# The order of the first two weight tiles in a seven-product FFN kernel: both P6 ahead of both P7, and the third tile's first sum made by a transfer

## The chip, the cores and the metric

The kernel runs on one core of one Trainium2 chip. Its time is the device time of one execution in microseconds (us); lower is better. A kernel's time is the median of several executions. One execution of it was recorded by the hardware profiler, and the trace of that one gives all durations, waits and starts below. Starts in the trace are counted from the beginning of the profiled span.

## What is computed

One decoder layer on a sequence of 1024 rows of 1024 numbers (float32): a pooling mixer, then a feed-forward network with a short causal convolution. Cut to what the change touches, the reference is:

```python
def conv_ffn(x, w_in, conv_w, conv_b, w_out):
    h = causal_depthwise_conv(x @ w_in, conv_w, conv_b)   # 3 taps
    val, gate = jnp.split(h, 2, axis=-1)
    return (jax.nn.silu(gate) * val) @ w_out

x = x + pool_mixer(rms_norm(x, norm_mix_g), ...)
x = x + conv_ffn(rms_norm(x, norm_ffn_g), ...)
```

x is 1024 by 1024, w_in 1024 by 5632 (2816 values and 2816 gates), w_out 2816 by 1024. The change touches only the product with w_in and what follows it up to the gated result.

## The kernel before, in words

**Stages.** First the pooling mixer and the norms (rows of x in eight blocks, up to some 75 us of the span). Then the product with w_in: 22 weight tiles n = 0 to 21, each of 128 value columns and the 128 gate columns that belong to them; the result of each tile is gated and written to HBM (`g_dram`). Last the product with w_out (L722 on).

**Seven products in place of eight.** A weight tile is a 2 by 2 block matrix (A11, A12 for the value columns, A21, A22 for the gate columns; each 128 by 512), and the normed rows are one as well (B11 to B22). The kernel uses a Strassen-Winograd scheme: sums S1 to S4 of the tile's blocks, sums T1 to T4 of the rows' blocks, and seven products P1 to P7 (the table STEPS, L421). Each takes one A side and one B side into one PSUM bank:

P1 = A11, B11 (bank X); P6 = S2, T2 (Y); P5 = S1, T1 (Z); P2 = A12, B21 (X, added to P1); P7 = S3, T3 (Y, added to P6); P3 = S4, B22 (Z, added to P5); P4 = A22, T4 (Y, added again).

Every float32 operand is split in a high and a low part (`split`, L91, for the A side: a copy on ACT at L93, then a subtraction on DVE at L94; `split_n`, L351, for the B side, the same at L353 and L354). One product is 12 matmuls on TensorE (PE): four pieces of 128 rows by three pairs of parts (`product`, L413).

**Evictions.** Between the products of one tile, DVE reads the banks (`step`, L430): q2 = Y after P6 minus q1 (L447), half of `hb` = r minus Y after P7 (L455), the other half = q1 minus Y after P4 (L460), `ha` from Z and q2 (L449). A product that adds to a bank can't start before DVE has read what it needs of the bank's state: P7 of a tile waits for its q2, P4 for its first half of `hb`. The tile `hb` (the gate half, 128 by 1024) has one buffer (L454, bufs=1), and so has `ha` (the value half).

**Gating** (`conv` L462, `gated` L472). For `ha` and then `hb`: one ACTIVATE on ACT (L465) and two SCALAR_TENSOR_TENSOR on DVE (L466, L467, the second on the first's output); then Silu on ACT (L476), a multiplication on DVE (L477) and a write to HBM.

**Weight sums** (`sums_in` L373, `prep_in` L391). A tile's raw weights are loaded into one of two `win` buffers by one 1 MB transfer on SP's queue (L362), which must wait until the tile two before it has made its last split, that of A22. S3 starts as another load of A11 (L381). Then GpSimd's queue (POOL) issues transfers that add in flight (L376): first A21 onto S3, then A22 onto A21 (which gives S1). S2 is A11 + S1, in place of A11: tiles 0 and 1 get it by a transfer too, all others by one addition on DVE (L368 by way of L399). S4 is A12 + S2.

**What sets the order.** The list `events` (L480 to L482) is the order in which products are asked for; `prep_event(k + LOOK)` asks for the operand splits five events ahead. A scheduler in the recording layer turns the program into one fixed queue for each engine, and each queue is worked off in order. For tiles 0 and 1 the list interleaves, since T2, T3 and T4 become ready only while these tiles are multiplied (L596 to L609); from tile 2 on it runs tile by tile in the order of STEPS.

Of the kernel before, what the change touches and what calls it, by code (L numbers as in the profile page):

```python
# [11 lines left out]
ALU = mybir.AluOpType  # L12
# [35 lines left out]
NH = 512  # L48
# [4 lines left out]
def woven(t):  # L53
    return t.rearrange("p (a b) -> p b a", a=2)
# [6 lines left out]
def halved(t, n=2):  # L61
    return t.rearrange("p (a b) -> p a b", a=n)
# [3 lines left out]
def trunk_kernel(ctx: ExitStack, tc: tile.TileContext, x, consts, par, rows, pool_w, w_in, w_out, out):  # L66
# [47 lines left out]
    def affine(t, src, op, fill, base, pattern, step):  # L114
        nc.gpsimd.affine_select(out=t, in_=src, compare_op=op, fill=fill, base=base, pattern=pattern, channel_multiplier=step)
# [21 lines left out]
    for g, w in enumerate(WINDOWS):  # L137

        m = band[:, g, :]
# [28 lines left out]
    marks = {}  # L168
# [153 lines left out]
    nops = {}  # L322
# [28 lines left out]
    def split_n(t, src, cols=None, ks=slice(None)):  # L351
        h, l = (t[:, i, ks] if cols is None else t[:, i].rearrange("p k (a s) -> p k a s", a=2)[:, :, :, cols] for i in range(2))
        hi = nc.scalar.activation(h, src, AF.Copy).ins  # L353
        return hi, nc.vector.tensor_tensor(l, src, h.bitcast(F32), ALU.subtract).ins  # L354
# [3 lines left out]
    raws, sums, aops = {}, {}, {}  # L358
# [11 lines left out]
    def tmp(name):  # L370
        return work.tile([P, NH], F32, tag="sum", name=name, bufs=3)

    def sums_in(n, step):  # L373

        def more(out, a):
            nc.gpsimd.dma_start(out, a, accum_op=ALU.add)  # L376

        a11, a12, a21, a22 = (raws[n][:, i, k * NH : (k + 1) * NH] for i in range(2) for k in range(2))
        if step == 0:
            s3 = sums[n, "S3"] = tmp(f"S3_{n}")  # L380
            nc.sync.dma_start(s3, w_in[order[n]][:, 0, :NH])  # L381
            more(s3, a21)
        if step == 0 and n > 1 or step == 2:
            more(a21, a22)
        if step == 1:
            sums[n, "S2"] = a11
            more(a11, a21)
            sums[n, "S4"] = a12
            more(a12, a11)

    def prep_in(n, op):  # L391
        a11, a12, a21, a22 = (raws[n][:, i, k * NH : (k + 1) * NH] for i in range(2) for k in range(2))
        if op in ("S1", "S2") and (n, "S3") not in sums:
            s3 = sums[n, "S3"] = tmp(f"S3_{n}")
            add(s3, a11, a21)
            add(a21, a21, a22)
        if op in ("S2", "S4") and (n, "S2") not in sums:
            sums[n, "S2"] = a11
            add(a11, a21, a11)  # L399
        if op == "S4" and (n, "S4") not in sums:  # L400
            add(a12, a12, a11)
        if op == "S3":
            src = sums[n, "S3"]
        else:
            src = {"A11": a11, "A12": a12, "S1": a21, "A22": a22, "S2": a11, "S4": a12}[op]
        log = []
        aops[n, op] = split(src, f"{op}s_{n}", log)
        marks[op, n] = log[0]
        if op == "A22" and n + 2 < NF:
            load_in(n + 2)  # L410
            sums_in(n + 2, 0)

    def product(bank, a, b, opens):  # L413
        m = 0
        for k in range(4):
            ks = slice(k * P, (k + 1) * P)
            for i, l in ((0, 0), (0, 1), (1, 0)):
                nc.tensor.matmul(bank, a[:, i, ks], woven(b[:, l, k, :]), start=opens and m == 0, stop=m == 11, skip_group_check=not opens)  # L418
                m += 1

    STEPS = {  # L421
        "P1": ("A11", "B11", "X"), "P6": ("S2", "T2", "Y"), "P5": ("S1", "T1", "Z"), "P2": ("A12", "B21", "X"),
        "P7": ("S3", "T3", "Y"), "P3": ("S4", "B22", "Z"), "P4": ("A22", "T4", "Y"),
    }
    banks, hid = {}, {}

    def small(tag, name, bufs):
        return work.tile([P, NH], F32, tag=tag, name=name, bufs=bufs)

    def step(n, p):  # L430
        a, b, z = STEPS[p]
        opens = p in ("P1", "P6", "P5")
        if opens:
            pool = ps_x if z == "X" else ps_yz
            banks[n, z] = pool.tile([P, NH], F32, tag=z, name=f"{z}{n}")
        bank = banks[n, z]
        product(bank, aops.pop((n, a)), nops[b], opens)
        tt = nc.vector.tensor_tensor
        if p == "P1":
            hid[n, "q1"] = small("q1", f"q1_{n}", 2)  # L440
            nc.scalar.activation(hid[n, "q1"], bank, AF.Copy, scale=-1.0)
        elif p == "P2":
            hid[n, "a"] = work.tile([P, S], F32, tag="ha", name=f"ha{n}", bufs=1)
            nc.scalar.activation(hid[n, "a"][:, :NH], bank, AF.Copy)
        elif p == "P6":
            hid[n, "q2"] = tmp(f"q2_{n}") if n < 2 else late.tile([P, NH], F32, tag="q2", name=f"q2_{n}", bufs=2)
            tt(hid[n, "q2"], bank, hid[n, "q1"], ALU.subtract)  # L447
            if n < 2:
                tt(hid[n, "a"][:, NH:], banks[n, "Z"], hid[n, "q2"], ALU.add)  # L449
        elif p == "P5":  # L450
            hid[n, "r"] = left.tile([P, NH], F32, tag="r", name=f"r_{n}", bufs=2)
            tt(hid[n, "r"], hid[n, "q1"], bank, ALU.subtract)  # L452
        elif p == "P7":
            hid[n, "b"] = late.tile([P, S], F32, tag="hb", name=f"hb{n}", bufs=1)  # L454
            tt(hid[n, "b"][:, NH:], hid[n, "r"], bank, ALU.subtract)  # L455
        elif p == "P3":
            if n >= 2:
                tt(hid[n, "a"][:, NH:], bank, hid[n, "q2"], ALU.add)
        else:
            tt(hid[n, "b"][:, :NH], hid[n, "q1"], bank, ALU.subtract)  # L460
# [11 lines left out]
    def gated(n):  # L472
        j = order[n]
        val = conv(hid[n, "a"], j, "val")
        gate = conv(hid[n, "b"], NF + j, "gate")
        nc.scalar.activation(gate, gate, AF.Silu)  # L476
        nc.vector.tensor_tensor(val, val, gate, ALU.mult)  # L477
        nc.sync.dma_start(g_dram[j], val)

    events = [(n, p) for p in ("P1", "P2") for n in range(2)]  # L480
    events += [(n, p) for p in ("P5", "P3") for n in range(2)] + [(n, p) for n in range(2) for p in ("P6", "P7", "P4")]
    events += [(n, p) for n in range(2, NF) for p in STEPS]  # L482
    LOOK = 5

    def prep_event(k):
        if k < len(events):
            n, p = events[k]
            prep_in(n, STEPS[p][0])

    def event(k):  # L490
        if k >= 4:
            prep_event(k + LOOK)
        n, p = events[k]
        step(n, p)
        if p == "P4":
            gated(n)
# [47 lines left out]
    for j in range(2, NS + 4):  # L544
# [17 lines left out]
        if j in (4, 6):  # L562
            load_in(j // 2 - 2)
            sums_in(j // 2 - 2, 0)
        if j in (5, 6):
            with tc.issue_after(biased[j - 1]):
                sums_in(j - 5, 2)
# [6 lines left out]
        if j in (8, 10, 11):  # L574
            event((8, 10, 11).index(j))
# [15 lines left out]
    halves = [slice(0, 2), slice(2, 4)]  # L591
    t1, t3, b22, t4 = n2f[:, lo, s0], n2f[:, lo, s1], n2f[:, hi, s1], n2f[:, hi, s0]
    event(3)
    with tc.issue_after(marks["T1"][0]), tc.issue_after(marks["T1"][1]):
        event(4)
        for ks in halves:  # L596
            split_n(nops["B22"], b22[:, ks], ks=ks)
    event(5)
    event(6)
    for ks in halves:  # L600
        nc.vector.scalar_tensor_tensor(b22[:, ks], b22[:, ks], -1.0, t1[:, ks], op0=ALU.mult, op1=ALU.subtract)  # L601
        split_n(nops["T2"], b22[:, ks], ks=ks)
    event(7)
    event(8)
    for ks in halves:
        split_n(nops["T3"], t3[:, ks], ks=ks)
    for ks in halves:
        nc.vector.scalar_tensor_tensor(t4[:, ks], b22[:, ks], -1.0, t4[:, ks], op0=ALU.mult, op1=ALU.subtract)
        split_n(nops["T4"], t4[:, ks], ks=ks)  # L609
    mid.close()  # L610
    late_stack = ExitStack()
    late = late_stack.enter_context(tc.tile_pool(name="late", bufs=1, side="right"))
    for k in range(9, len(events)):
        event(k)
    late_stack.close()

# [118 lines left out]
    for k in range(-SLOOK, len(oevents)):  # L735
        p, f = oevents[k + SLOOK] if k + SLOOK < len(oevents) else (None, 0)
# [8 lines left out]
        with tc.issue_after(lasts[-1]) if lasts else nullcontext():  # L745
# [12 lines left out]
            p, f = oevents[k]  # L758
# [9 lines left out]
        set_, opens = chains[p]  # L768
# [6 lines left out]
        if k >= len(oevents) - TAIL:  # L775
# [5 lines left out]
            z = halved(zs["z21", 3])[:, :, NH // 4 :]  # L781
# [5 lines left out]
        for i, g, c, bank in steps:  # L787
            a, b = oops[p, g]
# [89 lines left out]
```

## Time and profile before

| what | us |
|---|---|
| median of 3 runs (lowest to highest) | 669.31 (669.21 to 669.54) |
| the profiled execution's own time | 670.47 |
| its span, first to last instruction | 668.8 |
| PE busy in the span | 662.6 (99%) |
| DVE busy | 569.0 (85%) |
| ACT busy | 339.4 (51%) |
| POOL busy | 52.1 (8%) |

So 1.67 us of the profiled execution lie outside its span. PE is the TensorE matmul, PEld its weight load, DVE VectorE, ACT ScalarE, POOL GpSimd, SP SyncE (it issues transfers). In a timeline a row gives start, time from the first instruction's start to the last one's end, engine, source line, operation, out<-in, how many instructions are merged into the row, and in brackets the engine's idle time ahead of it and what ended it. Names in the trace are without numbers, so the second q stands as q as well. A matmul's record is 0.38 us long and overlaps the next one: where PE is fed without a gap, they start 0.216 us apart.

### The profile page before, as it was taken

What the parts mean: (1) busy time and instruction counts of PE and PEld (TensorE: products, weight loads), DVE (VectorE), ACT (ScalarE), POOL (GpSimd) and SP (SyncE); (2) the same over time, 40 slices, a digit from 0 to 9 for tenths busy, and PEclk for the clock granted to TensorE, in tenths of its full rate; (3) what the DMA queues carried; (4) which work ended last, traced back from release to release, by engine and by line L of the source; (5) the groups of instructions that cost most, each with busy time, mean ns of one, the idle gap of its engine ahead of it and who ended that gap; (6) DMA issues with size and microseconds to landing.
All of it is one profiled execution on the core that took longest, in us unless ns stands there. A gap on an engine that the chain in (4) does not pass through costs nothing.

```text
span 668.8 us, 8723 instructions
## 1 busy us (share of the span) xinstructions
PE 662.6 (99%) x3156; PEld 577.6 (86%) x3156; DVE 569.0 (85%) x841; ACT 339.4 (51%) x517; POOL 52.1 (8%) x79
## 2 busy tenths in 40 slices
PE   9999999999999999999999999999999999999997
PEld 7889878888888888888888888888888888888886
DVE  4699999998888888888888888887987988999995
ACT  5687656554544544444545454454554444444441
POOL 4032020111001111111011101100000000000000
PEclk9999999999999999999999999999999999999999
DMA  7999253544444444444444444429999710122131
GB/s 242 345 264 219 83 137 126 172 144 124 128 135 108 124 137 141 141 136 126 133 141 131 113 135 134 111 93 331 354 323 342 293 52 0 62 96 81 62 126 64
DMA packets 42356, 103.85 MB, mean 155 GB/s; under 512 B 4773, under 2 KB 6729, under 8 KB 39497
## 3 DMA queue, kind: packets, MB, share of 16 engines
q1 hardware_dynamic: 34464, 87.55, 37.2%
q0 software_dynamic: 7696, 15.22, 13.2%
q10 hardware_dynamic: 152, 0.53, 0.3%
q8 instruction: 25, 0.41, 0.2%
q14 instruction: 19, 0.15, 0.1%
HBM read 68.66 MB, written 19.93 MB: 132 GB/s over the span
## 4 chain that ended last, share of the span: by engine, by line
PE 93%; DVE 3%; DMA 2%; ACT 1%; issue 1%; SPq 0%; ACTq 0%; DVEq 0%
PE oP L792 29%; PE Y L418 25%; PE X L418 17%; PE Z L418 16%; PE psy L299 4%; DMA x<-in_x_dram 2%; PE psd L203 1%; PE pst L334 1%; DVE T L354 1%; ACT junk_a L180 0%; DVE n2f L601 0%; ACT B L353 0%; DVE oBP L94 0%; PE psy L304 0%; ACT oBP L93 0%
## 5 line engine op out<-in xcount | busy, mean ns | idle before, releaser
L792 PE MATMUL oP<-oBP,oAP 128*128 128x512 f32 (+1 forms) x924 | 198.9, 378 | 0.1
L792 PEld LDWEIGHTS oP<-oBP,oAP 128*128 128x128 f32 x924 | 174.0, 189 | 25.0 <-DVE oBP L94 0.5
L418 PE MATMUL X<-B,A11s 128*128 128x512 f32 x264 | 61.5, 380 | 0.0
L418 PE MATMUL Y<-T,S3s 128*128 128x512 f32 x264 | 60.8, 380 | 0.4 <-DVE q L447 0.4
L418 PE MATMUL Y<-T,A22s 128*128 128x512 f32 x264 | 60.9, 380 | 0.0
L418 PE MATMUL Z<-T,S1s 128*128 128x512 f32 x264 | 60.8, 379 | 0.0
L418 PE MATMUL X<-B,A12s 128*128 128x512 f32 x264 | 60.6, 379 | 0.0
L418 PE MATMUL Y<-T,S2s 128*128 128x512 f32 x264 | 60.6, 379 | 0.0
L418 PE MATMUL Z<-B,S4s 128*128 128x512 f32 x264 | 60.5, 379 | 0.0
L418 PEld LDWEIGHTS Y<-T,S3s 128*128 128x128 f32 x264 | 49.7, 189 | 8.2 <-DVE q L447 1.2
L418 PEld LDWEIGHTS Y<-T,A22s 128*128 128x128 f32 x264 | 49.7, 189 | 7.9 <-DVE hb L455 0.6
L418 PEld LDWEIGHTS Z<-T,S1s 128*128 128x128 f32 x264 | 49.8, 189 | 7.5 <-DVE T L354 0.4
L418 PEld LDWEIGHTS Z<-B,S4s 128*128 128x128 f32 x264 | 49.8, 189 | 7.3 <-DVE r L452 0.3
L418 PEld LDWEIGHTS Y<-T,S2s 128*128 128x128 f32 x264 | 49.9, 189 | 7.1
L418 PEld LDWEIGHTS X<-B,A11s 128*128 128x128 f32 x264 | 49.7, 189 | 7.3 <-DVE A11s L94 0.4
L418 PEld LDWEIGHTS X<-B,A12s 128*128 128x128 f32 x264 | 49.8, 189 | 7.0
L93 ACT ACTIVATE oBP<-blk 128x512 fp32r<-128x512 f32 x53 | 33.1, 625 | 44.2 <-PE oP L792 30.7
L476 ACT ACTIVATE gate<-gate 128x1024 f32<-128x1024 f32 x22 | 23.2, 1056 | 49.3 <-DVE gate L467 49.3
L93 ACT ACTIVATE oAP<-blk 128x512 fp32r<-128x512 f32 x55 | 34.1, 620 | 19.3 <-DVE blk L365 16.8
L94 DVE TENSOR_TENSOR oBP<-blk,oBP 128x512 fp32r<-128x512 f32 x53 | 36.5, 688 | 8.6 <-ACT oBP L93 6.6
L94 DVE TENSOR_TENSOR oAP<-blk,oAP 128x512 fp32r<-128x512 f32 x55 | 37.7, 685 | 2.6 <-ACT oAP L93 2.6
L466 DVE SCALAR_TENSOR_TENSOR val<-ha,par_sb,val 128x1023 f32<-128x1023 f32 x22 | 28.2, 1283 | 13.2 <-ACT val L465 12.5
(134 smaller groups left out, 959.5 us busy)
## 6 DMA issues: line engine op xcount, KB each, us to landing
win<-in_w_in_dram SPq DMA_DIRECT2D x22, 1024.0 KB, 4.8
g_dram<-val SPq DMA_DIRECT2D x22, 512.0 KB, 2.6
blk<-g_dram SPq DMA_DIRECT2D x33, 256.0 KB, 5.3
blk<-in_w_out_dram SPq DMA_DIRECT2D x31, 256.0 KB, 5.6
win<-win POOLq DMA_DIRECT2D x26, 256.0 KB, 3.7
S<-in_w_in_dram SPq DMA_DIRECT2D x22, 256.0 KB, 3.4
S<-win POOLq DMA_DIRECT2D x22, 256.0 KB, 4.2
A12s<-g_dram SPq DMA_DIRECT2D x22, 256.0 KB, 5.3
```

The lines of the kernel that those rows point to most:

```text
L93: nc.scalar.activation(t[:, 0, :], src, AF.Copy)
L94: m = nc.vector.tensor_tensor(t[:, 1, :], src, t[:, 0, :].bitcast(F32), ALU.subtract)
L203: m = nc.tensor.matmul(ps[:, c * P : (c + 1) * P], src[:, c * P : (c + 1) * P], weights[:, c // 2, :], start=True, stop=True)
L299: m = nc.tensor.matmul(o, dh[:, c, :], wps[:, c, :], start=c % 4 == 0, stop=j >= BY_DMA and c % 4 == 3, skip_group_check=True)
L334: nc.tensor.transpose(ps[:, c * P : (c + 1) * P], n2[:, c * P : (c + 1) * P], ident)
L354: return hi, nc.vector.tensor_tensor(l, src, h.bitcast(F32), ALU.subtract).ins
L418: nc.tensor.matmul(bank, a[:, i, ks], woven(b[:, l, k, :]), start=opens and m == 0, stop=m == 11, skip_group_check=not opens)
L466: nc.vector.scalar_tensor_tensor(t[:, 1:], src[:, : S - 1], w[1], t[:, 1:], op0=ALU.mult, op1=ALU.add)
L476: nc.scalar.activation(gate, gate, AF.Silu)
L792: nc.tensor.matmul(bank, a[:, u, i * P : (i + 1) * P], woven(b[:, v, :])[:, c.start // 2 : c.stop // 2, :], start=opens and first, stop=g ...
```

## The change

The program does the same arithmetic, but for S2 of tile 2. Its parts:

1. **Order of events.** After the P3 of both tiles, events 8 to 13 were P6, P7, P4 of tile 0 and then P6, P7, P4 of tile 1. Now they are P6 of tile 0, P6 of tile 1, P7 and P4 of tile 0, P7 and P4 of tile 1. The splits of S2 of both tiles are asked for accordingly earlier.
2. **The third tile's P1** is put on PE's list right after event 10, P7 of tile 0 (`multiply(2, "P1")`); its eviction stays where it was. Its A11 split is asked for ahead of the split of T3 (`prep_event(9 + LOOK)` ahead of event 8).
3. **S2 of tile 2 by a transfer.** `sums_in(2, 3)` adds S1 onto A11 by one more transfer on POOL's queue, right behind the one that makes S1; the addition on DVE for tile 2 (L399) falls away.
4. **Gate's half first.** For tiles 0 and 1, the addition that makes the second half of `ha` moved from behind P6's eviction to behind P7's (the first half of `hb`), and the splits for events 15, 16 and 19 are asked for behind it.

The diff:

```diff
--- before.py
+++ after.py
@@ -382,9 +382,10 @@
             more(s3, a21)
         if step == 0 and n > 1 or step == 2:
             more(a21, a22)
-        if step == 1:
+        if step in (1, 3):
             sums[n, "S2"] = a11
             more(a11, a21)
+        if step == 1:
             sums[n, "S4"] = a12
             more(a12, a11)
 
@@ -427,14 +428,19 @@
     def small(tag, name, bufs):
         return work.tile([P, NH], F32, tag=tag, name=name, bufs=bufs)
 
-    def step(n, p):
+    def multiply(n, p):
         a, b, z = STEPS[p]
         opens = p in ("P1", "P6", "P5")
         if opens:
             pool = ps_x if z == "X" else ps_yz
             banks[n, z] = pool.tile([P, NH], F32, tag=z, name=f"{z}{n}")
+        product(banks[n, z], aops.pop((n, a)), nops[b], opens)
+
+    def step(n, p):
+        a, b, z = STEPS[p]
+        if (n, a) in aops:
+            multiply(n, p)
         bank = banks[n, z]
-        product(bank, aops.pop((n, a)), nops[b], opens)
         tt = nc.vector.tensor_tensor
         if p == "P1":
             hid[n, "q1"] = small("q1", f"q1_{n}", 2)
@@ -444,15 +450,18 @@
             nc.scalar.activation(hid[n, "a"][:, :NH], bank, AF.Copy)
         elif p == "P6":
             hid[n, "q2"] = tmp(f"q2_{n}") if n < 2 else late.tile([P, NH], F32, tag="q2", name=f"q2_{n}", bufs=2)
-            tt(hid[n, "q2"], bank, hid[n, "q1"], ALU.subtract)
-            if n < 2:
-                tt(hid[n, "a"][:, NH:], banks[n, "Z"], hid[n, "q2"], ALU.add)
+            marks[f"q2_{n}"] = tt(hid[n, "q2"], bank, hid[n, "q1"], ALU.subtract).ins
         elif p == "P5":
             hid[n, "r"] = left.tile([P, NH], F32, tag="r", name=f"r_{n}", bufs=2)
             tt(hid[n, "r"], hid[n, "q1"], bank, ALU.subtract)
         elif p == "P7":
             hid[n, "b"] = late.tile([P, S], F32, tag="hb", name=f"hb{n}", bufs=1)
-            tt(hid[n, "b"][:, NH:], hid[n, "r"], bank, ALU.subtract)
+            m = tt(hid[n, "b"][:, NH:], hid[n, "r"], bank, ALU.subtract).ins
+            if n < 2:
+                with tc.issue_after(m):
+                    tt(hid[n, "a"][:, NH:], banks[n, "Z"], hid[n, "q2"], ALU.add)
+                    for k in ((10, 11), (14,))[n]:
+                        prep_event(k + LOOK)
         elif p == "P3":
             if n >= 2:
                 tt(hid[n, "a"][:, NH:], bank, hid[n, "q2"], ALU.add)
@@ -478,7 +487,7 @@
         nc.sync.dma_start(g_dram[j], val)
 
     events = [(n, p) for p in ("P1", "P2") for n in range(2)]
-    events += [(n, p) for p in ("P5", "P3") for n in range(2)] + [(n, p) for n in range(2) for p in ("P6", "P7", "P4")]
+    events += [(n, p) for p in ("P5", "P3") for n in range(2)] + [(n, p) for n, p in ((0, "P6"), (1, "P6"), (0, "P7"), (0, "P4"), (1, "P7"), (1, "P4"))]
     events += [(n, p) for n in range(2, NF) for p in STEPS]
     LOOK = 5
 
@@ -488,7 +497,7 @@
             prep_in(n, STEPS[p][0])
 
     def event(k):
-        if k >= 4:
+        if k >= 4 and k not in (9, 10, 11, 14):
             prep_event(k + LOOK)
         n, p = events[k]
         step(n, p)
@@ -601,16 +610,21 @@
         nc.vector.scalar_tensor_tensor(b22[:, ks], b22[:, ks], -1.0, t1[:, ks], op0=ALU.mult, op1=ALU.subtract)
         split_n(nops["T2"], b22[:, ks], ks=ks)
     event(7)
+    prep_event(9 + LOOK)
+    sums_in(2, 3)
     event(8)
     for ks in halves:
         split_n(nops["T3"], t3[:, ks], ks=ks)
+    event(9)
     for ks in halves:
         nc.vector.scalar_tensor_tensor(t4[:, ks], b22[:, ks], -1.0, t4[:, ks], op0=ALU.mult, op1=ALU.subtract)
         split_n(nops["T4"], t4[:, ks], ks=ks)
     mid.close()
     late_stack = ExitStack()
     late = late_stack.enter_context(tc.tile_pool(name="late", bufs=1, side="right"))
-    for k in range(9, len(events)):
+    event(10)
+    multiply(2, "P1")
+    for k in range(11, len(events)):
         event(k)
     late_stack.close()
```

What the scheduler makes of it can be read from the queues. First DVE's queue, from the eviction of tile 1's P6 (`q2_1`) to the eviction of tile 1's P7 (`hb1`). Names end in the tile's number and a buffer's; a name with `s_2` is the split of an operand of tile 2, `val0` and `gate22` are the convolutions of tile 0. Before:

```order
L447 TENSOR_TENSOR q2_1_1004<-Y1_991,q1_1_751 128x512
L94 TENSOR_TENSOR S2s_2_961<-win2_847,S2s_2_961 128x512
L466 SCALAR_TENSOR_TENSOR val0_977<-ha0_779,par_sb_126,val0_977 128x1023
L94 TENSOR_TENSOR S1s_2_988<-win2_847,S1s_2_988 128x512
L460 TENSOR_TENSOR hb0_958<-q1_0_684,Y0_913 128x512
L467 SCALAR_TENSOR_TENSOR val0_977<-ha0_779,par_sb_126,val0_977 128x1022
L94 TENSOR_TENSOR A12s_2_1007<-win2_847,A12s_2_1007 128x512
L466 SCALAR_TENSOR_TENSOR gate22_981<-hb0_958,par_sb_126,gate22_981 128x1023
L449 TENSOR_TENSOR ha1_820<-Z1_853,q2_1_1004 128x512
L467 SCALAR_TENSOR_TENSOR gate22_981<-hb0_958,par_sb_126,gate22_981 128x1022
L94 TENSOR_TENSOR S3s_2_1024<-S3_2_849,S3s_2_1024 128x512
L455 TENSOR_TENSOR hb1_1022<-r_1_866,Y1_991 128x512
```

The same stretch of DVE's queue in the changed program (its lines are numbered differently: L453 is P6's eviction, L459 P7's, L469 P4's, L475 and L476 the convolution, L462 the moved addition):

```order
L459 TENSOR_TENSOR hb0_973<-r_0_838,Y0_917 128x512
L462 TENSOR_TENSOR ha0_779<-Z0_825,q2_0_930 128x512
L94 TENSOR_TENSOR S2s_2_976<-win2_865,S2s_2_976 128x512
L453 TENSOR_TENSOR q2_1_949<-Y1_936,q1_1_751 128x512
L94 TENSOR_TENSOR S1s_2_979<-win2_865,S1s_2_979 128x512
L475 SCALAR_TENSOR_TENSOR val0_1008<-ha0_779,par_sb_126,val0_1008 128x1023
L94 TENSOR_TENSOR A12s_2_1019<-win2_865,A12s_2_1019 128x512
L469 TENSOR_TENSOR hb0_973<-q1_0_684,Y0_917 128x512
L476 SCALAR_TENSOR_TENSOR val0_1008<-ha0_779,par_sb_126,val0_1008 128x1022
L475 SCALAR_TENSOR_TENSOR gate22_1012<-hb0_973,par_sb_126,gate22_1012 128x1023
L476 SCALAR_TENSOR_TENSOR gate22_1012<-hb0_973,par_sb_126,gate22_1012 128x1022
L459 TENSOR_TENSOR hb1_1034<-r_1_860,Y1_936 128x512
```

The split of S2 of tile 2 now stands one place ahead of `q2_1`, where it stood one behind, and the second step of val0's convolution and both of gate22's now follow one another up to `hb1`.

Then PE's queue from tile 0's P6 on (a row is one product or a piece of one; Y0, Y1, Y2 are the Y banks of tiles 0, 1 and 2). Before:

```order
L418 MATMUL Y0_913<-T2_792,S2s_0_805 128x512 x12
L418 MATMUL Y1_991<-T2_792,S2s_1_868 128x512 x6
L418 MATMUL Y0_913<-T3_793,S3s_0_822 128x512 x12
L418 MATMUL Y1_991<-T2_792,S2s_1_868 128x512 x6
L418 MATMUL X2_1055<-B11_155,A11s_2_943 128x512 x12
L418 MATMUL Y0_913<-T4_795,A22s_0_844 128x512 x12
L418 MATMUL Y1_991<-T3_793,S3s_1_889 128x512 x12
L418 MATMUL Y2_1079<-T2_792,S2s_2_961 128x512 x12
L418 MATMUL Z2_1097<-T1_156,S1s_2_988 128x512 x8
L418 MATMUL Y1_991<-T4_795,A22s_1_904 128x512 x12
```

And in the changed program:

```order
L419 MATMUL Y0_917<-T2_792,S2s_0_805 128x512 x12
L419 MATMUL Y1_936<-T2_792,S2s_1_822 128x512 x12
L419 MATMUL Y0_917<-T3_793,S3s_0_844 128x512 x12
L419 MATMUL X2_982<-B11_155,A11s_2_904 128x512 x12
L419 MATMUL Y0_917<-T4_795,A22s_0_862 128x512 x12
L419 MATMUL Y1_936<-T3_793,S3s_1_889 128x512 x12
L419 MATMUL Y2_1079<-T2_792,S2s_2_976 128x512 x12
L419 MATMUL Z2_1097<-T1_156,S1s_2_979 128x512 x3
L419 MATMUL Y1_936<-T4_795,A22s_1_908 128x512 x12
```

All twelve matmuls of tile 1's P6 now stand ahead of tile 0's P7, and three matmuls of tile 2's P5, where there were eight, stand ahead of tile 1's P4. The third tile's P1 (X2) stood ahead of tile 0's P4 in the program before too.

On ACT's queue the copy that opens S2's split of tile 2 stood behind the first step of val0's convolution; now val0's first step stands behind the copies for S2, S1 and A12 of tile 2. On POOL's queue one more transfer stands between tile 2's second one (which makes S1) and tile 3's first.

## The prediction, made before the changed kernel ran

> **What bounds the kernel now.** I read the page first, then the busy time by stretch, then the timelines of the engines around the change.
>
> ```profile
> span 668.8 us, 8723 instructions
> PE 662.6 (99%) x3156; PEld 577.6 (86%) x3156; DVE 569.0 (85%) x841; ACT 339.4 (51%) x517; POOL 52.1 (8%) x79
> ```
>
> PE is the bound over the whole span: 662.6 of 668.8 us. A change of order can win only where PE waits, and loses where it makes PE wait. The next view gives two stretches: the one whose order the change touches, from tile 0's P6 to tile 3's P6, and the rest of the w_in product. Columns: length, then busy time and instructions of PE, PEld, DVE, ACT, POOL, then granted clock, DMA share, GB/s.
>
> ```profile
> 85.25:123.42 38.17, 37.74 (x169) 31.19 (x168) 37.97 (x47) 21.44 (x28) 5.15 (x6) 1.00 0.47 134
> 123.42:465.47 342.05, 342.05 (x1586) 299.54 (x1585) 283.13 (x361) 166.36 (x228) 29.19 (x34) 1.00 0.48 138
> ```
>
> The second stretch holds 132 products of 12 matmuls: 342.05 / 1584 = 0.2159 us for one matmul, 2.59 for a product, with no wait. The first holds 14 products, 168 matmuls, which would take 36.28 us; it took 38.17. So **PE waits 1.89 us there, and that is all the change can win**. DVE is busy 37.97 of these 38.17 us: here it is DVE that sets the pace, and every moment in which DVE's queue stands still is paid.
>
> ```profile
> 85.25 4.05 PE L418 MATMUL Y<-T,S2s 128*128 128x512 f32 x18
> 89.71 2.86 PE L418 MATMUL Y<-T,S3s 128*128 128x512 f32 x12 [0.41 <-DVE q L447]
> 92.40 1.46 PE L418 MATMUL Y<-T,S2s 128*128 128x512 f32 x6
> 93.70 3.04 PE L418 MATMUL X<-B,A11s 128*128 128x512 f32 x12
> 96.74 2.83 PE L418 MATMUL Y<-T,A22s 128*128 128x512 f32 x12
> 99.41 2.75 PE L418 MATMUL Y<-T,S3s 128*128 128x512 f32 x12
> ```
>
> PE's timeline shows where. 18 matmuls from 85.25 end their slots at 89.14; P7 of tile 0 begins at 89.71 and its 12 matmuls take 2.69 in place of 2.59: 0.67 us lost to q2, the 0.10 being the refill after a wait. From 93.70 to 99.41 stand 24 matmuls, 5.18 us, in 5.71: 0.53 lost, to the A11 split of tile 2 and to T4. The other 0.69 lies in four waits between 106 and 121.
>
> **The change, part by part.** *Both P6 first*: PE has six more matmuls (1.30 us) between P6 and P7 of tile 0, more than the 0.67 that it waits for q2. That wait goes. *A11's split earlier*: of the 0.53 I keep 0.2 for T4, whose copies are only reshuffled. The third tile's P1 stood ahead of P4 already, so that edit by itself moves nothing. *The addition on DVE*: one slot less for DVE, 0.60 us (below). So far a gain of about 1.
>
> What comes in its place is **a DVE queue that waits for a transfer**: the split of S2 of tile 2 now stands ahead of q2 of tile 1, and its data comes by a third transfer in a row on POOL's queue. P7 of tile 1 can't start before that q2. I follow the chain with these rows of POOL's queue and SP's, and the page's median times to landing:
>
> ```profile
> 79.87 7.27 SPq L362 DMA_DIRECT2D win<-in_w_in_dram  x2
> ...
> 85.34 0.85 POOL L376 DMA_DIRECT2D S<-win  x1 [24.89 <-DMA win<-in_w_in_dram]
> 89.36 0.86 POOL L376 DMA_DIRECT2D win<-win  x1 [3.16 <-DVE T L354]
> 92.24 0.85 POOL L376 DMA_DIRECT2D S<-win  x1 [2.02 <-DMA win<-in_w_in_dram]
> 96.06 0.86 POOL L376 DMA_DIRECT2D win<-win  x1 [2.96 <-DVE win L368]
> 117.53 0.85 POOL L376 DMA_DIRECT2D S<-win  x1 [20.61 <-DVE win L368]
> 122.12 0.86 POOL L376 DMA_DIRECT2D win<-win  x1 [3.74 <-DVE S3s L94]
> ...
> win<-win POOLq DMA_DIRECT2D x26, 256.0 KB, 3.7
> S<-win POOLq DMA_DIRECT2D x22, 256.0 KB, 4.2
> ```
>
> and these of DVE and ACT:
>
> ```profile
> 79.16 0.68 DVE L94 TENSOR_TENSOR A22s<-win,A22s 128x512 fp32r<-128x512 f32 x1
> 79.76 0.68 DVE L94 TENSOR_TENSOR S2s<-win,S2s 128x512 fp32r<-128x512 f32 x1
> ...
> 88.98 0.68 DVE L447 TENSOR_TENSOR q<-Y,q 128x512 f32<-128x512 f32 x1
> ...
> 96.52 0.68 DVE L447 TENSOR_TENSOR q<-Y,q 128x512 f32<-128x512 f32 x1
> ...
> 99.64 0.68 DVE L460 TENSOR_TENSOR hb<-q,Y 128x512 f32<-128x512 f32 x1
> 100.24 1.28 DVE L467 SCALAR_TENSOR_TENSOR val<-ha,par_sb,val 128x1022 f32<-128x1022 f32 x1
> 101.43 0.68 DVE L94 TENSOR_TENSOR A12s<-win,A12s 128x512 fp32r<-128x512 f32 x1
> ```
> ```profile
> 95.43 1.25 ACT L465 ACTIVATE val<-ha,par_sb 128x1024 f32<-128x1024 f32 x1 [1.82 <-DVE T L354]
> 96.59 0.61 ACT L93 ACTIVATE S2s<-win 128x512 fp32r<-128x512 f32 x1
> 97.10 0.62 ACT L93 ACTIVATE S1s<-win 128x512 fp32r<-128x512 f32 x1
> 97.63 0.61 ACT L93 ACTIVATE A12s<-win 128x512 fp32r<-128x512 f32 x1
> ...
> 100.35 1.24 ACT L465 ACTIVATE gate<-hb,par_sb 128x1024 f32<-128x1024 f32 x1 [1.59 <-DVE hb L460]
> ...
> 117.59 0.61 ACT L93 ACTIVATE S1s<-win 128x512 fp32r<-128x512 f32 x1
> ```
>
> A DVE row of 0.68 gives way to the next after 0.60 (79.16 to 79.76), one of 1.28 after 1.19 (100.24 to 101.43), ACT's copies after 0.52; who waits for a result starts 0.05 after its end (q ends at 89.66, P7 starts at 89.71).
>
> 1. Tile 2's load waits for the split of A22 of tile 0, and one more split (S2 of tile 1) stands ahead of that on DVE: 79.87 + 0.60 = 80.47. The three transfers that add follow: the first 5.47 after the load as before, 85.94; from one to the next that needs it 4.02 (85.34 to 89.36), so 89.96 and 93.98, landing 3.7 later: **S2 is there at 97.68**.
> 2. ACT copies S2 at 97.73 to 98.34, S1 from 98.25, A12 from 98.78. DVE splits S2 at 98.39; q2 of tile 1 runs from 98.99 to 99.67; P7 of tile 1 can start at 99.72, with refill 99.82. PE has done its 60 matmuls from 85.25 by 98.20, with the 0.2 kept by 98.40. **First new wait: 1.42 us.**
> 3. PE then has 27 matmuls (P7 of tile 1, P6 of tile 2, three of P5), 5.83 us, to 105.65. P4 of tile 1 waits for `hb1`. ACT's first step of val0 stands behind the three copies: 99.30 to 100.55. DVE: S1's split from 99.59, val0 at 100.60, A12's split at 101.79, `hb0` at 102.39 to 103.07, val0's second step at 102.99. ACT makes gate22 from 103.12 to 104.36; DVE runs its first step from 104.41 to 105.69, its second, on the first's output, from 105.74 to 107.01. `hb1` goes into the one buffer which that second step reads, so it runs from 107.06 to 107.74, and P4 starts at 107.79, with refill 107.89. **Second new wait: 2.24 us**, and it does not depend on when S2 lands: both ends of it hang on q2 of tile 1.
> 4. Of the four late waits one is now inside the second, and the rest stay near: I keep 0.5.
>
> Sum: 0.2 + 1.42 + 2.24 + 0.5 = 4.36, against 1.89 before: **+2.47 us**. DVE's side agrees: it reaches S2's split some 0.5 ahead of the 96.52 at which q2 of tile 1 began (the addition's 0.60 gone), so at about 96.0, and stands still to 98.39, and then 0.4 for val0 and 0.2 around gate22: 3.0 idle in place of 0.2, less the addition of 0.60, +2.2. From 123.42 on PE had no wait, with DVE busy 283.13 of 342.05 us, so nothing is won back.
>
> Moved with no price: the load for S3 of tile 3 and tile 3's two transfers queue behind the new one, but the latter were done at about 100 (96.06 + 3.7) and tile 3's S1 was copied at 117.59.
>
> The unknown is the landing of S2. Intervals on POOL run from 3.82 (92.24 to 96.06) to 4.59 (117.53 to 122.12), and this row bounds the landing (transfers of `win` from 76 to 140 us, loads included):
>
> ```profile
> DMA to landing us min/median/max: 3.3/3.8/4.9
> ```
>
> Twice 3.82 and 3.3 gives 96.88, so +1.67; twice 4.59 and the 4.2 of `S<-win` gives 99.32, so +4.1. I take the quiet 4.02 and 3.7, of the same tile's own transfers. [...]
>
> **The rivals.** *Hidden transfer, not slower.* If S2 lands by about 96, DVE does not stand still at it: the first new wait is 0. Then val0's chain starts 1.3 earlier against PE and the second wait shrinks to about 0.95: 0.2 + 0 + 0.95 + 0.5 = 1.65, 669.1 us. It takes three transfers 0.55 us quicker each than the rows; even the shortest rows make 96.88. 0.08. *Crowded transfers.* S3 of tile 3 is now loaded right ahead of tile 2's weights, and tile 3's load (the second of SP's row) waits for a split that moves back, so it runs beside the additions. At the upper bounds: +4.1, 673.4. 0.13. *The clock drops.* PE has never been idle for over 0.7 us in this stage at a granted 1.00. If a gap of 2.2 us makes the clock fall to half for one product, that costs 2.59 more: 674.4. 0.04. [...] *That the change doesn't do what it says* is ruled out by the queues. *Faster*: were both new waits to vanish, 0.7 would stay, 668.1, and even that is within the bound below; 0.02.
>
> **How the numbers follow.** The forecast, 0.73, is 669.31 + 2.47 = 671.8 us on the median; the profiled execution, 670.47 for a span of 668.8, would become 672.9. Its own range is 671.0 to 673.4. The range given, 670.7 to 673.4, holds it and the crowded case; the hidden transfer, the clock and the faster end lie outside. A measurement of this kernel tells from no change about 0.2%, 1.34 us: slower by more are forecast, crowding and clock, less their lowest tail, 0.88; within it the hidden transfer and that tail, 0.10; faster 0.02.
>
> **What would show it.** In the changed profile PE waits for q (L453) at the P7 of tile 1, near 98, over 1 us, and for hb (L459) at P4 of tile 1, near 106, for 2.2; DVE's idle time goes to ACT's copy of S2, and that to a transfer `win<-win`; the 0.67 at P7 of tile 0 is gone. I am wrong if S2's copy starts before 96.5, if P4 of tile 1 waits for under 1 us, or if waits appear after 125 us.

## The result: 674.1 us for 669.4

| | us | runs |
|---|---|---|
| before, median (lowest to highest) | 669.42 (668.97 to 670.33) | 6 |
| after | 674.09 (672.32 to 675.47) | 6 |
| ratio after to before | 1.0068, 95% interval 1.0052 to 1.0084 | |
| profiled execution of after; its span | 674.86; 673.1 | 1 |

Two executions in the experiments below, one of 998.74 us (the order with A11's split) and one of 1424.27 us (the order alone), lie so far above all others of their kernels that the medians leave them out.

Slower, as forecast, but by 4.67 us where 2.47 was forecast, and above the range. PE's timeline of the changed kernel, over the stretch in question, shows all of it:

```profile
84.70 5.34 PE L419 MATMUL Y<-T,S2s 128*128 128x512 f32 x24
90.13 2.86 PE L419 MATMUL Y<-T,S3s 128*128 128x512 f32 x12
92.82 2.75 PE L419 MATMUL X<-B,A11s 128*128 128x512 f32 x12
95.63 2.83 PE L419 MATMUL Y<-T,A22s 128*128 128x512 f32 x12
100.39 2.86 PE L419 MATMUL Y<-T,S3s 128*128 128x512 f32 x12 [1.94 <-DVE q L453]
103.09 2.75 PE L419 MATMUL Y<-T,S2s 128*128 128x512 f32 x12
105.68 0.81 PE L419 MATMUL Z<-T,S1s 128*128 128x512 f32 x3
108.46 4.51 PE L419 MATMUL Y<-T,A22s 128*128 128x512 f32 x12 [1.98 <-DVE hb L459]
112.77 2.18 PE L419 MATMUL Z<-T,S1s 128*128 128x512 f32 x9
114.79 2.75 PE L419 MATMUL X<-B,A12s 128*128 128x512 f32 x12
```

From 84.70 to 114.79 there are 108 matmuls, 23.31 us at 0.2158, in 30.09: 6.78 us lost, where the whole stretch before lost 1.89. The difference, 4.89, less 0.55 by which PE entered this stretch sooner (84.70 for 85.25), is the span's 4.3. The 6.78 split as follows, each from a start less what PE had to do before it (with 0.10 of refill): 0.35 at P7 of tile 0 (90.13), 0.29 at its P4 (95.63), **2.21 at P7 of tile 1** (ready at 98.28, refilled by 100.49), **2.24 at P4 of tile 1** (ready at 106.32), and **1.7 in the matmuls behind that**: twelve that take 4.31 us in place of 2.59. Nothing is lost later. The two brackets name the two waits foretold, q at L453 and hb at L459. For the last loss, the busy time by stretch, cut at the steps of the clock's record; columns as in the prediction, the clock behind POOL's column:

```profile
95.85:99.27 3.41, 2.60 (x12) 1.93 (x11) 0.45 (x2) 0.88 (x2) 0.85 (x1) 1.00 0.90 153
99.27:102.68 3.41, 2.29 (x11) 2.02 (x12) 3.12 (x5) 1.93 (x3) 0.86 (x1) 1.00 0.32 55
...
106.09:109.50 3.41, 1.44 (x7) 0.94 (x6) 3.27 (x5) 1.80 (x2) 0.00 (x0) 1.00 0.00 0
109.50:112.92 3.41, 3.41 (x10) 2.70 (x9) 3.04 (x5) 3.41 (x6) 0.00 (x0) 0.50 0.43 167
112.92:116.33 3.41, 3.41 (x18) 2.98 (x17) 3.32 (x4) 1.59 (x2) 0.00 (x0) 1.00 0.53 145
```

The second wait lies inside the 3.41 us from 106.09, in which PE was busy 1.44 (42%), and in the next 3.41 us the granted clock is 0.50. The windows before that one are counted back from it; they are those of the record, for its three stretches of clock 1.00, 0.50 and 1.00 last 102.40, 3.41 and 559.79 us, which is 30, 1 and 164 times 3.413. The first wait is as long as the second, but cut in two by 99.27: the rows on both sides are 76% and 67% busy, and the clock behind them stays at 1.00. All six executions of the changed kernel have a mean clock of 0.997, which is what one such step makes (3.41 / 2 in 673 is 0.25%). Then the chain behind S2, from the queues of SP, POOL, ACT and DVE:

```profile
79.31 0.33 SPq L381 DMA_DIRECT2D S<-in_w_in_dram  x1
79.91 8.78 SPq L362 DMA_DIRECT2D win<-in_w_in_dram  x2
86.81 0.86 POOL L376 DMA_DIRECT2D S<-win  x1 [26.96 <-DMA win<-in_w_in_dram]
90.81 0.86 POOL L376 DMA_DIRECT2D win<-win  x1 [3.14 <-DMA S<-win]
94.96 0.86 POOL L376 DMA_DIRECT2D win<-win  x1 [3.29 <-DVE T L354]
```
```profile
98.38 0.63 ACT L93 ACTIVATE S2s<-win 128x512 fp32r<-128x512 f32 x1 [4.95 <-DMA win<-win]
...
99.96 1.24 ACT L474 ACTIVATE val<-ha,par_sb 128x1024 f32<-128x1024 f32 x1
```
```profile
87.04 0.69 DVE L94 TENSOR_TENSOR A11s<-win,A11s 128x512 fp32r<-128x512 f32 x1 [0.28 <-ACT A11s L93]
...
89.39 0.68 DVE L453 TENSOR_TENSOR q<-Y,q 128x512 f32<-128x512 f32 x1
...
99.05 0.69 DVE L94 TENSOR_TENSOR S2s<-win,S2s 128x512 fp32r<-128x512 f32 x1 [2.96 <-ACT S2s L93]
99.65 0.68 DVE L453 TENSOR_TENSOR q<-Y,q 128x512 f32<-128x512 f32 x1
...
106.34 1.28 DVE L476 SCALAR_TENSOR_TENSOR gate<-hb,par_sb,gate 128x1022 f32<-128x1022 f32 x1
107.72 0.69 DVE L459 TENSOR_TENSOR hb<-r,Y 128x512 f32<-128x512 f32 x1
```

From 98.38 on this is the chain of the prediction's steps 1 to 3, instruction by instruction (the two rows ahead of it belong to P7 of tile 0, and come up again below), with S2 at 98.33 in place of 97.68. Tile 2's load was issued 0.56 sooner than worked out, but the first addition (86.81) came 6.90 after it in place of 5.47. Right ahead of it, by 0.60, stands the load for S3 of tile 3; before, that load stood 3.5 ahead.

### The profile page after: what moved, and what is told of

Same layout as the page of the kernel before. It is cut to its first block, busy times and chain, and to the rows that moved or that the text cites. A ratio compares the mean times of both kernels' runs of the same rounds, so it can differ in the third digit from the quotient of the medians.

```text
span 673.1 us, 8725 instructions
## 1 busy us (share of the span) xinstructions
PE 663.3 (99%) x3156; PEld 578.9 (86%) x3156; DVE 569.4 (85%) x840; ACT 339.2 (50%) x517; POOL 53.1 (8%) x80
## 4 chain that ended last, share of the span: by engine, by line
PE 91%; DMA 3%; DVE 3%; ACT 2%; issue 0%; SPq 0%; ACTq 0%; DVEq 0%
PE oP L806 29%; PE Y L419 24%; PE X L419 17%; PE Z L419 15%; PE psy L299 4%; PE psd L203 1%; DMA x_edge<-in_x_dram 1%; PE pst L334 1%; DMA win<-in_w_in_dram 1%; DMA x<-in_x_dram 1%; ACT junk_a L180 0%; ACT B L353 0%; DVE oBP L94 0%; PE psy L304 0%; DVE A22s L94 0%
## 5 line engine op out<-in xcount | busy, mean ns | idle before, releaser
L419 PE MATMUL Y<-T,A22s 128*128 128x512 f32 x264 | 62.4, 387 | 2.0 <-DVE hb L459 2.0
L376 POOL DMA_DIRECT2D S<-win x22 | 19.2, 875 | 263.4 <-DMA win<-in_w_in_dram 232.2
```

## The experiments

Theory A: the landing of S2 is the cause, and whatever is queued behind its copy on ACT and its split on DVE pays. Rival B: the new order and the buffers make the waits. Apart from these, what makes the clock halve was in question. PE's waits below are worked out as above, over 168 matmuls (36.25 us) where nothing else is said.

**Parts taken out or done alone.** First, the addition on DVE put back (`if step == 1:` again, and no `sums_in(2, 3)`), all else as changed:

> The changed kernel without its third part: S2 of tile 2 is made by one addition on DVE again, all other parts stay. Theory A (the landing of the third transfer is the cause: DVE's and ACT's queues stand behind it): the wait of 2.2 us at P7 of tile 1 goes, that at P4 of tile 1 shrinks from 2.24 to about 1.1, and with no wait of 2 us the clock stays at 1.00. PE's waits from 85 us on come to about 1.7 in place of 6.8: 669.2 us, 668.6 to 669.9. Theory B (the buffers and the order make the waits: q2 of tile 1 behind the moved addition, hb1 behind both of gate22's steps in one buffer): both waits stay at 1.5 to 2.2 without the transfer, 671.5 to 674.

670.54 us (11 runs) against 669.60, ratio 1.0011 (1.0002 to 1.0019). Each against its own runs of before, the loss falls from 4.67 to 0.94: the transfer makes 3.7 of it, in this order. P7 of tile 1 has no wait, P4's is 0.99, the clock stays at 1.00, and B's waits don't appear. But the waits are 2.9, not 1.7: P7 of tile 0 alone has 0.88. PE's row at P4 of tile 1, which was ready at 105.03:

```profile
105.92 2.86 PE L418 MATMUL Y<-T,A22s 128*128 128x512 f32 x12 [0.73 <-DVE hb L458]
```

The transfer alone, in the old order:

```diff
+        if k == 9:
+            sums_in(2, 3)
```

> The kernel before with the third part alone: S2 of tile 2 by a third transfer, in the old order, in which q2 of tile 1 stands ahead of S2's split on DVE's queue. Theory A (a transfer costs what is queued behind its reader): the three waits before 97 us (0.68, 0.29, 0.24) stay or shrink, one wait of about 1.3 comes at P4 of tile 1, the late four shrink: waits of 2.2 in all in place of 1.9, 669.7 us, 669.2 to 670.5, clock 1.00. Theory B (the order and the buffers are the cause): no price, 669.4 within 0.3. A third way (the transfer slows the neighbouring transfers or ports wherever it stands): over 671.

670.23 us (11 runs) against 669.60, 1.0011 (1.0002 to 1.0020). The wait at P4 of tile 1 is there (1.28 and refill), waits of 2.4 in all. So the transfer costs 0.6 in the old order. There q2 of tile 1 stands ahead of S2's split on DVE, and the first step of val0 ahead of S2's copy (96.88) on ACT. The first addition, too, came 5.32 after the load, as S3's load stands 3.5 ahead of it. This run doesn't tell these three apart; a price wherever the transfer stands (over 671) it does rule out. ACT's and PE's rows:

```profile
94.09 1.25 ACT L466 ACTIVATE val<-ha,par_sb 128x1024 f32<-128x1024 f32 x1 [1.82 <-DVE T L354]
```
```profile
106.68 2.86 PE L419 MATMUL Y<-T,A22s 128*128 128x512 f32 x12 [1.12 <-DVE hb L456]
```

The order and A11's split ahead of T3's, without the transfer and without gate's half first (`events` as changed, `prep_event(9 + LOOK)` ahead of `event(8)`):

> The kernel before with the new order of events and the third tile's A11 split ahead of T3's, without the transfer and without gate's half first. Theory A: no queue stands behind a landing, so the order by itself wins part of the 0.68 at P7 of tile 0 and the 0.29 at the third tile's P1, and pays some of it back at P7 of tile 1: waits of about 1.4 in place of 1.9, 668.9 us, 668.4 to 669.4. Theory B (the order is the cause): a wait of over 1.5 at P7 of tile 1, 671 or more.

669.65 us (11 runs) against 669.60, 1.0003 (0.9993 to 1.0013): no measurable difference, where a gain was expected. DVE's queue and PE's say why:

```profile
87.14 0.69 DVE L94 TENSOR_TENSOR A11s<-win,A11s 128x512 fp32r<-128x512 f32 x1 [1.16 <-ACT A11s L93]
87.75 0.68 DVE L94 TENSOR_TENSOR A22s<-win,A22s 128x512 fp32r<-128x512 f32 x1
88.35 1.22 DVE L354 TENSOR_TENSOR T<-n2f,T 128x1024 fp32r<-128x1024 f32 x1
89.49 0.68 DVE L447 TENSOR_TENSOR q<-Y,q 128x512 f32<-128x512 f32 x1
```
```profile
90.23 2.86 PE L418 MATMUL Y<-T,S3s 128*128 128x512 f32 x12 [0.96 <-DVE q L447]
```

A11's split, moved ahead, waits 1.16 us for the same late load, with T3's split and q2 of tile 0 queued behind it. P7 of tile 0, ready at 89.10, waits 1.23 with refill: the 1.30 us of matmuls that the order puts ahead of it are eaten up.

**What holds P4 of tile 1.** The changed kernel with the splits of S2, S1 and A12 of tile 2 behind q2 of tile 1:

```diff
-                        prep_event(k + LOOK)
+                        with tc.issue_after(marks["q2_1"]) if n == 0 else nullcontext():
+                            prep_event(k + LOOK)
```

(and the same for A12's, asked for in event 12.)

> The changed kernel with the splits of S2, S1 and A12 of tile 2 put behind q2 of tile 1 on DVE's queue; the transfer and all else stay. The prediction's step 3 (both ends of the second wait hang on q2 of tile 1): P7 of tile 1 has no wait, P4's keeps its 2.24, so the sum falls by the first wait of 2.2: about 671.9 at most, and no half clock if only the two waits together made it. The rival (P4's end hangs on the landing of S2, by way of val0's first step on ACT behind the copies of S2, S1 and A12, and of DVE's queue up to hb1): P4 starts at about 108.5 as in the changed kernel, P7's wait of 2.2 is only moved there, one wait of 4.4 to 4.7; the time stays near 672.4 with the clock at 1.00, and near 674 if the clock halves for 3.4 us.

674.58 us (6 runs), 1.0072 (1.0059 to 1.0085). PE:

```profile
102.64 0.81 PE L419 MATMUL Z<-T,S1s 128*128 128x512 f32 x3
107.66 5.49 PE L419 MATMUL Y<-T,A22s 128*128 128x512 f32 x12 [4.20 <-DVE hb L459]
```

The first wait is gone and the second takes it over: 4.37 and refill. S2's copy started at 97.57 here and P4 at 107.66, 10.09 later; in the changed kernel 98.38 and 108.46, 10.08. P4 hangs on S2's landing, not on q2, and the rival written in the expectation holds. Nor is it q2's place that made the transfer cheap in the old order: here q2 stands ahead too, and val0's first step behind the three copies on ACT (99.15) as in the changed kernel, and nothing is won.

Then the landing itself. The changed kernel with S3's load of tile 3 behind tile 3's weights:

```diff
-            nc.sync.dma_start(s3, w_in[order[n]][:, 0, :NH])
+            with tc.issue_after(marks["load", 3]) if n == 3 else nullcontext():
+                nc.sync.dma_start(s3, w_in[order[n]][:, 0, :NH])
```

> The changed kernel with the load for S3 of tile 3 behind tile 3's weights on SP's queue, where it stood 0.6 us ahead of tile 2's. If that load lengthened tile 2's (first addition on POOL 6.90 us after the issue of the load in place of 5.47), the first addition comes 5.3 to 5.6 after the load again, S2's copy about 1.4 sooner, at 97.0 for 98.4 (by starts counted as in the changed kernel), and the sum of the two big waits falls by about that: 4.4 to about 3.0, 672.5 us, 671 to 673. If the time came from elsewhere (the other loads and writes at that time), nothing changes: 674 within 0.8. By the prediction's step 3 only the first wait would shrink, and the second stay at 2.24.

672.67 us (4 runs) against 669.52, 1.0046 (1.0032 to 1.0060). SP, POOL, ACT and PE:

```profile
79.19 7.28 SPq L362 DMA_DIRECT2D win<-in_w_in_dram  x2
```
```profile
84.51 0.86 POOL L376 DMA_DIRECT2D S<-win  x1 [25.55 <-DMA win<-in_w_in_dram]
```
```profile
96.82 0.64 ACT L93 ACTIVATE S2s<-win 128x512 fp32r<-128x512 f32 x1 [4.48 <-DMA win<-win]
```
```profile
83.97 5.34 PE L420 MATMUL Y<-T,S2s 128*128 128x512 f32 x24
...
98.83 2.86 PE L420 MATMUL Y<-T,S3s 128*128 128x512 f32 x12 [1.06 <-DVE q L454]
...
104.12 0.81 PE L420 MATMUL Z<-T,S1s 128*128 128x512 f32 x3
106.90 2.86 PE L420 MATMUL Y<-T,A22s 128*128 128x512 f32 x12 [1.98 <-DVE hb L460]
```

The first addition comes 5.32 after the load, S2's copy 1.56 sooner than in the changed kernel, the first wait is 1.33, the second still 2.24, and again 10.08 lie between S2's copy and P4. So the load for S3, issued right ahead, did lengthen the way to the first addition (6.90 with it there). The sum of the two waits fell by 0.9 and not by 1.4: PE too was in this stretch 0.73 sooner (83.97 for 84.70), so against PE S2 came only 0.83 sooner.

The changed kernel with the addition for `ha` back behind q2, ahead of hb0's first half:

> The changed kernel without its fourth part's main step: the addition that makes the second half of ha stands behind q2 again, ahead of hb0's first half, so that q2 of tile 1 can run without waiting for it; S2 still comes by the transfer. Theory A (whatever stands behind S2's copy on ACT and its split on DVE pays): q2 of tile 1 runs early and P7 of tile 1 has no wait, but A12's split, whose copy stands behind S2's on ACT, now stands ahead of hb0, and one wait of about 5 us comes at P4 of tile 0, with the clock at half for two windows behind it: 675 to 677. Theory B (gate's half first, with q2 of tile 1 behind the moved addition, is the cause): most of the loss of 4.7 goes, 669.5 to 671.

676.40 us (4 runs) against 669.60, 1.0095 (1.0080 to 1.0111). DVE and PE:

```profile
101.44 0.69 DVE L94 TENSOR_TENSOR A12s<-win,A12s 128x512 fp32r<-128x512 f32 x1 [4.37 <-ACT A12s L93]
```
```profile
102.88 5.46 PE L419 MATMUL Y<-T,A22s 128*128 128x512 f32 x12 [5.17 <-DVE hb L461]
```

Theory A's number: q2 of tile 1 is early, and another instruction behind the landing pays, 5.34 at P4 of tile 0. B by itself is out: without the transfer its waits don't appear. But with the transfer, the order decides what stands behind the landing.

**The clock.** Extra matmuls (`B11` by itself, into a bank that nobody reads) ahead of P4 of tile 1 fill the second wait, or ahead of P7 the first (nine there, and three more ahead of P4); they are work beyond the reference's, so the times aren't compared.

```diff
+        if (n, p) == (1, "P4"):
+            multiply(2, "P6")
+            behind = tc.issue_after(fill("fill2", (2, "P6"), 12))
```

> The changed kernel with twelve extra matmuls (B11 by itself, into a bank of their own that nobody reads) on PE's queue ahead of P4 of tile 1, where the second wait was; tile 2's P6 stands ahead of them. The first wait of 2.2 us stays. What matters are the clock's records and the matmuls after each wait, not the total. If the clock halves by the busy share of a 3.413 us window (under about half busy), a gap of 2.2 us halves it only where it lies within one window: with the windows as in the changed kernel, whose first wait was split between two, no half clock, mean clock 1.00 in most executions. If any gap of over 2 us halves it, the half clock comes near 101 to 105 in every execution. If it takes two gaps in a row, none comes in any execution.

> The changed kernel with nine extra matmuls of the same kind ahead of P7 of tile 1, where the first wait was, and three ahead of P4 of tile 1; the second wait of 2.2 us stays. By the busy share of a window: the half clock comes for one window of 3.413 us after the second wait where that lies within one window, as in the changed kernel. By two gaps in a row: no half clock in any execution, mean clock 1.00. By any gap of over 2 us: the half clock in every execution.

675.43 and 676.30 us (4 runs each). In both profiles the remaining wait lay inside one window and the clock halved in the next. First the run with the second wait filled, then that with the first filled:

```profile
97.49:100.90 3.41, 1.55 (x8) 1.04 (x7) 2.04 (x4) 2.80 (x4) 0.86 (x1) 1.00 0.43 73
100.90:104.31 3.41, 3.41 (x10) 2.70 (x9) 3.41 (x4) 1.04 (x1) 0.00 (x0) 0.50 0.45 77
```
```profile
106.41:109.82 3.41, 1.46 (x7) 0.94 (x6) 3.27 (x5) 1.66 (x3) 0.00 (x0) 1.00 0.00 0
109.82:113.23 3.41, 3.41 (x10) 2.66 (x9) 3.41 (x6) 3.41 (x6) 0.00 (x0) 0.50 0.51 145
```

But not in every execution: the mean clock was 0.997 in two of four with the second filled and in three of four with the first filled, else 0.999 or 1.00. So it doesn't take two gaps. Nor does every gap of 2.2 us do it: the first one of the changed kernel, cut in two, didn't. What the waits and windows were in the executions without a half clock isn't on record. The run with S3's load later fits, whose second wait of 2.24 was cut by a window's end:

```profile
102.88:106.30 3.41, 2.04 (x10) 1.45 (x8) 3.15 (x4) 1.67 (x4) 0.00 (x0) 1.00 0.00 0
106.30:109.71 3.41, 2.81 (x13) 2.49 (x14) 3.41 (x6) 3.40 (x5) 0.00 (x0) 1.00 0.18 63
```

60% and 82% busy, no half clock; one of its four executions has 0.997.

**The order alone, and a better version.** The events' order and nothing else:

> The kernel before with the new order of events and nothing else: A11's split of the third tile stays where it was. In the run with the order and A11's split ahead, DVE stood idle for 1.16 us at that split, since its data had not landed, and P7 of tile 0 waited 1.23 us behind it. If that is the price of A11's place, the wait at P7 of tile 0 goes here, one of 0.3 to 1.0 stands at the third tile's P1, later ones as before: waits of 1.0 to 1.5 in place of 1.9, 668.8 us, 668.4 to 669.4. If the order itself delays q2 of tile 0 (DVE has as much to do ahead of it), P7 of tile 0 waits 0.6 to 1.2 here too: 669.5 to 670.

670.91 us (10 runs) against 669.52, 1.0019 (1.0010 to 1.0028): slower, not faster. No trace shows where these ten wait. The trace is of one more execution:

> The new order of events alone a second time, for a profile in which the clock is undisturbed; its time of 670.93 against 669.52 says that waits of about 3.3 in place of 1.9 stand somewhere. If T3's splits and q2 of tile 0 stand behind a split of tile 2 whose data lands late (A11's, as in the run with the order and A11's split ahead), the wait stands at P7 of tile 0; if A11's own product pays (its split is late where it stands), it stands at the third tile's P1, at about 95, with 1 to 1.8 us.

672.32 us in its one execution, 0.87 above the highest of the ten, so its waits need not be theirs. The third tile's P1 waits 0.96, and P4 of tile 0 a further 1.79, which was not expected, behind an addition on DVE that waits for a landing. That landing was late because POOL's second addition came 6.71 after its first (87.99 and 94.70; in the changed kernel 4.00), which it waits for: the first took 6.16 from issue to landing. Tile 3's 1 MB load was issued 0.77 ahead of it here (87.22), and 1.5 to 1.6 behind it in the changed kernel (88.36 for 86.81) and in the kernel before (86.81 for 85.34); whether that is the cause was not tried.

Last, the order with A11's split ahead, S3's load later as above, and T4's first steps held behind q2 of tile 0 (`tc.issue_after(marks["q2_0"])`); no transfer for S2, no gate's half first:

> The kernel before with the new order of events and A11's split ahead of T3's, the load for S3 of tile 3 behind tile 3's weights, and T4's first steps held behind q2 of tile 0. In the run without the last two, DVE stood idle for 1.16 us at A11's split and P7 of tile 0 waited 1.23, while tile 2's first addition came 7.77 after the issue of its load. If S3's load makes that lateness, it comes 5.3 to 5.5 after the load here, DVE's idle time at A11's split is under 0.2, and P7 of tile 0 waits under 0.7: waits of 1.0 to 1.8 in all, 668.4 to 669.6 us, a little ahead of the kernel before or level with it. If the lateness has another cause, 669.8 to 670.5.

668.54 us (11 runs) against 669.60, ratio 0.9987 (0.9979 to 0.9996): **faster than both kernels**. DVE:

```profile
84.25 1.22 DVE L354 TENSOR_TENSOR T<-n2f,T 128x1024 fp32r<-128x1024 f32 x1
85.39 0.69 DVE L94 TENSOR_TENSOR A11s<-win,A11s 128x512 fp32r<-128x512 f32 x1
```

No idle time at A11's split; the first addition 5.33 after the load (79.76 and 85.09); waits of 0.7 in place of 1.9. The two edits beyond the order with A11's split were not tried apart.

## Why the prediction had the two waits right and the time wrong

The step that failed is the clock. The sum has no term for it, and it measured 1.7 us; without it the median would be 672.4, inside the range. S2's landing was mis-sized besides, 0.65 late. Part by part:

- *Both P6 first: "That wait goes."* It failed in part: 0.35 of the 0.67 stayed. The step counted PE's six matmuls and not DVE's queue, where A11's split (0.60, and 0.28 idle ahead of it for its data) had moved ahead of q2 of tile 0. With the addition back on DVE it was 0.88. P4 of tile 0, where T4 was priced at 0.2, lost 0.29.
- *Step 1, S2 at 97.68.* Mis-sized: 98.33. The term that failed is "the first 5.47 after the load as before", which took 6.90. S3's load 0.6 ahead made it: 6.8 to 7.8 in the runs that have it there, 5.3 in both that move it away. The two steps of 4.02 were 4.00 and 4.15, the landing 3.4 for 3.7.
- *Step 2, the first wait.* The mechanism was right: 2.21 for 1.42, of which 0.65 is S2's lateness.
- *Step 3, the second wait.* 2.24, as worked out. That "both ends of it hang on q2 of tile 1" was right only while q2 itself stands behind S2: with q2 freed, P4 still came 10.1 us behind S2's copy.
- *Step 4, 0.5 for late waits.* None were left, as with the transfer alone, where the clock stayed up; what took them away was not tried.
- *The clock, 0.04.* This is the step that put the time outside the range. It stood among the rivals, at nothing in the sum. The price was near (2.59 for one product; 1.7 measured), the chance was not: all six executions have the mean clock of 0.997. The sentence that PE had never been idle for over 0.7 us at a granted 1.00 said nothing about 2.2. That the clock would fall to half, and for one product, was an assumption that no row of before shows; the changed kernel's record shows 0.50 for one step of 3.41 us, behind a window with PE busy 1.44 of 3.41 us (42%), and 43% and 45% were enough in the runs with one wait filled.

The sum: 0.35 + 0.29 + 2.21 + 2.24 + 1.7 = 6.8 for 4.36. That it is 4.4 without the clock and S2's lateness is partly luck: 0.44 too little at the start and 0.5 too much for the late waits nearly cancel. *Crowded transfers* and *The clock drops* were priced as alternatives; both came, each in part.

## What to carry to other kernels

Before an instruction is put ahead in an in-order queue, look up when its data lands, and read off everything that stands behind it: the transfer cost 0.6 us in the old order and 3.7 in the new one. Look at every engine's queue: with only q2 moved ahead of the reader nothing was won; val0's first step still stood behind it on ACT. Price a transfer's landing from rows with the same neighbours on the queue: with a 256 KB load issued 0.6 us ahead of tile 2's 1 MB load, the first addition came 6.8 to 7.8 us after that load, else 5.3 to 5.5. In the changed kernel one wait of 2.24 us on TensorE cost another 1.7 in clock, so a forecast with such a wait needs that case in its range.

## What the hardware showed

- The clock's record moves in steps of 3.41 us (stretches of 30, 1 and 164 of them in the changed kernel). From full clock, a window with PE busy 42%, 43% or 45% was followed by one at half clock, and so were two less busy ones, with 18% (0.60, the first row below) and 0% (0.00 of the 3.41 from 98.39, ahead of the fourth); windows with 60%, 67% and 76% were not. If the busy share decides, these windows put the limit between 45 and 60%, an estimate.
- Once at half, the clock stayed there behind windows of 59% and 68%, and came back behind one that was busy throughout (3.41 of 3.41). With S2's splits behind q2 (first three rows) and with `ha`'s addition early (last two), it stayed at half for two windows, though PE was busy 2.03 and 2.33 of 3.41 in the first of them:

```profile
102.86:106.27 3.41, 0.60 (x3) 0.19 (x1) 3.26 (x4) 2.21 (x3) 0.00 (x0) 1.00 0.00 0
106.27:109.68 3.41, 2.03 (x5) 1.67 (x6) 3.31 (x6) 2.79 (x4) 0.00 (x0) 0.50 0.07 23
109.68:113.09 3.41, 3.41 (x10) 2.69 (x9) 2.05 (x3) 2.78 (x5) 0.00 (x0) 0.50 0.57 221
```
```profile
101.80:105.21 3.41, 2.33 (x6) 1.91 (x7) 3.38 (x6) 0.75 (x1) 0.72 (x1) 0.50 0.45 77
105.21:108.63 3.41, 3.41 (x10) 2.69 (x9) 1.49 (x2) 0.60 (x1) 0.00 (x0) 0.50 0.00 0
```

- A 256 KB load issued 0.6 us ahead of a 1 MB load on the same queue lengthened the way from the big load's issue to the first addition: 6.8 to 7.8 us in eight kernels that have it there, 5.3 to 5.5 in four that don't.
